# Twenty-two placements and orders for the two parts of a weight unit, in the half-steps of a macaron layer

## The chip, the cores and the metric

The kernel runs on one core of one Trainium2 chip (trn2). The metric is the device time of one execution in microseconds (us), the median of three runs. The engines of the core are named as in the profile: PE is the matrix engine and PEld its weight loads, DVE the vector engine, ACT the scalar engine, POOL the general engine, SP and ACT also issue the transfers.

## What is computed

One layer: a half-step SwiGLU feed-forward network (below: the first half-step), a token mixer of forgetting and stick-breaking attention with gated branches, and a second half-step of the same kind as the first. 16 meta tokens stand ahead of the 256 tokens and are dropped at the end. Everything is float32. Cut to the half-steps:

```
def _rmsnorm(x, gain):
    y = x32 * lax.rsqrt(jnp.mean(x32 * x32, axis=-1, keepdims=True) + RMS_EPS)
    return (y * gain).astype(x.dtype)
def _swiglu(x, w_gate, w_up, w_down):
    return (jax.nn.silu(x @ w_gate) * (x @ w_up)) @ w_down
...
h = h + 0.5 * _swiglu(_rmsnorm(h, ffn1_norm), ffn1_w_gate, ffn1_w_up, ffn1_w_down)
h = h + _hybrid_mixer(_rmsnorm(h, mix_norm), ...)
h = h + 0.5 * _swiglu(_rmsnorm(h, ffn2_norm), ffn2_w_gate, ffn2_w_up, ffn2_w_down)
```

The model width is 2048, the inner width 5632, so gate, up and down of one half-step hold 3 x 2048 x 5632 weights.

## The kernel before

**Parts.** A float32 product is made of three products of a faster type (float32r). Each operand is split into a high part (rounded) and a low part (the rest); high by high, high by low and low by high are added up in one accumulator, and low by low is left out. For weights the parts are the tiles `wh` and `wl`: ACT rounds (`act.activation(hi, src, AF.Copy)`, L164), DVE subtracts (L165).

**Units.** All weights are cut into units of 1024 columns by 128 partitions, 512 KB each: two blocks of 128 rows (`n` = 2) by 512 output features where a block is 512 wide. There are 264 units in the first half-step, then those of the mixer, then 264 in the second half-step. SP loads a unit up to six units ahead (`raw`, five buffers), `split_unit` makes its parts up to two units ahead (three buffers each of `wh` and `wl`, 4096 bytes a partition), and `products` (L917) issues its matmuls at L944. The order of the program is this loop; the lanes of generators that `tick()` moves on put the other work (norms, attention, transposes) between the matmuls. A scheduler of the language sets the final order from the program's order and its own estimate of when inputs are there.

**First half-step: by feature.** A matmul has 128 weights columns as stationary operand and 272 tokens (256 and 16 meta) of the activations as moving one. A unit has four outputs (`j`), two blocks of rows (`i`) and three terms, 24 matmuls. The four outputs have one of the eight accumulator banks each. The three terms of one `i` follow each other: `wh` with the activations' high part, `wh` with their low part, `wl` with their high part. The activations' parts lie in tiles of 2 x 2 x 272 (`tile_of`, L204): block, part, token. One row of 272 elements is 1088 bytes, 64 more than a multiple of 256, so the four rows of such a tile begin 0, 64, 128 and 192 bytes past a multiple of 256, counted from the tile's begin.

**Second half-step: by token.** Here the activations are stationary (128 tokens of a high or low part) and 512 weight columns are moving: two outputs, two blocks, three terms, 12 matmuls a unit, in the order (activations high, `wh`), (high, `wl`), (low, `wh`). The activations' tiles are 2 x 2 x 256 here, rows of 1024 bytes: all four begin at a multiple of 256 from the tile's begin.

**The mixer** has both kinds: by-feature blocks for queries, keys and values, and by-token blocks for the gates and the branches. The gates read the normalized activations in the tile of 272-token rows; the branches read the attention's outputs in tiles of 256-token rows. So the gates and the branches are the same matmuls (128 stationary columns, 512 moving ones) with other distances between the operands' begins.

**Where the tiles lie.** The built program has the activations' tiles (4352 bytes a buffer, 17 x 256), the `wh` and `wl` buffers and each of their halves all at one and the same rest from a multiple of 256 (192 bytes past it). In what follows the **distance** of a matmul is the rest by 256 of the moving operand's begin less the stationary one's. It is 0, 64, 0, 128, 192, 128 for the six matmuls of one output in the first half-step, and 0 for all of the second half-step and of the branches.

**The start.** `first_start` and `first_products` (L906) run ahead of the loop; the transposes there need the unit matrix `ident`, which POOL makes; `identr` and `onesr` are copies of `ident` and `ones` in float32r, made later (L136, L137).

**The end.** `down2` (L832) adds each finished output to the residual (DVE, L838) and sends it out (L841). In the last block each output is worked off in two halves.

Of the kernel before, what the change touches and what calls it, by code (L numbers as in the profile page):

```python
# [32 lines left out]
SPLIT_BUFS = 3  # L33
LOAD_AHEAD = 6
SPLIT_AHEAD = 2


class Block:
# [9 lines left out]
def hybrid_layer(ctx: ExitStack, tc: tile.TileContext, x, meta_tokens, ffn1_norm, ffn1_w_gate, ffn1_w_up,  # L48
# [47 lines left out]
            tick()  # L96


    ident = const([P, P], F32, "ident")
    make_identity(nc, ident)  # L100
    ones = const([P, P], F32, "ones")
    nc.gpsimd.memset(ones[:], 1.0)
    eps_c = const([P, 1], F32, "eps")
    nc.gpsimd.memset(eps_c[:], EPS)
    grow = const([64, P], F32, "grow")
    grow1 = const([16, P], F32, "grow1")
    nc.scalar.dma_start(grow1[:], ffn1_norm.rearrange("o (k p) -> (o k) p", p=P))
    for i, g in enumerate((ffn1_norm, mix_norm, ffn2_norm)):
# [7 lines left out]
    def tables():  # L116
        return tc.keep_in_program_order(act.preload_act_table_set(LN_EXP)).ins

    gcol1 = const([P, 16], F32, "gcol1")
    gcol = const([P, 64], F32, "gcol")  # L120
    gq = const([P, 8], F32, "gq")

    identr = const([P, P], F32R, "identr")
    onesr = const([P, P], F32R, "onesr")
# [5 lines left out]
    def other_constants():  # L130
        yield 8
        g_ps = aux()
        pe.transpose(g_ps[:, :64], grow[:], ident[:64, :64])
        dve.tensor_copy(gcol[:], g_ps[:, :64])
        dve.tensor_scalar(gq[:], gcol[:, 48:56], SCALE, None, op0=ALU.mult)
        tc.keep_in_program_order(dve.tensor_copy(identr[:], ident[:]))  # L136
        tc.keep_in_program_order(dve.tensor_copy(onesr[:], ones[:]))  # L137
        tc.keep_in_program_order(dve.tensor_scalar(negone[:], ones[:], -1.0, None, op0=ALU.mult))
# [54 lines left out]
    class Norm:  # L193
# [53 lines left out]
        def by_feature(self):  # L247

            n, ps = self.n, aux()
            pe.matmul(ps[:, :n], ones[:], self.acc[:, :n], start=True, stop=True)  # L250
# [43 lines left out]

    def first_gains():
        g_ps = aux()
        pe.transpose(g_ps[:, :16], grow1[:], ident[:16, :16])
        dve.tensor_copy(gcol1[:], g_ps[:, :16])

    def first_meta():  # L300
        p = aux()
        for h in range(2):
            pe.transpose(p[:, h * P:(h + 1) * P], ms[:, h, :], ident[:])
        t = p[:, :2 * P].rearrange("p (k t) -> p k t", t=NM)
        dve.tensor_tensor(mgain, t, gcol1[:].unsqueeze(2).to_broadcast([P, KT, NM]), op=ALU.mult)
        return t

    def first_transposes(c):
        ps = [aux(), aux()]
        for i in range(2):  # L310
            for j in range(2):
                pe.transpose(ps[i][:, j * P:(j + 1) * P], xs[c][:, j, i * P:(i + 1) * P], ident[:])  # L312
        return ps

    def first_parts(kt, p):
# [51 lines left out]
            act.activation(s[:], xs[c][:, j, :], AF.Square, accum_out=sums[:, j, c:c + 1])  # L367

    def meta_squares():
        dve.tensor_reduce(msel, ident[:].rearrange("p (k t) -> p t k", t=NM), axis=AX.X, op=ALU.add)  # L370
# [4 lines left out]
    def first_factors():  # L375
# [12 lines left out]
        rsqrt_newton(a[:], y[:], half[:])  # L388
        diag = temp([P, NT], F32, "half")
        for j in range(2):  # L390
            dve.tensor_scalar(diag[:, j * P:(j + 1) * P], ident[:], a[:, j:j + 1], None, op0=ALU.mult)
# [3 lines left out]
        pe.matmul(p[:, :NR], ones[:], diag[:, :NR], start=True, stop=True)  # L395
# [8 lines left out]
    def turn(u, dest, t0):  # L404

        yield 6
        for j0 in range(0, 4, 2):
            p = aux()
            for j in range(2):
                for i in range(2):  # L410
                    c = (j0 + j) * P
                    pe.transpose(p[:, (2 * j + i) * P:(2 * j + i + 1) * P], u[:, i, c:c + P], ident[:])  # L412
# [144 lines left out]
    def values(v):  # L557
        pv = aux()
        for i in range(3):
            pe.transpose(pv[:, i * P:(i + 1) * P], v[:, i * P:(i + 1) * P], ident[:])  # L560
# [83 lines left out]
    def fox_attend(h, t, parts):  # L644
# [23 lines left out]
        for kt in range(3):  # L668
            d = pb if kt == 2 else pa
            for i in range(2):  # L670
                c = (kt % 2) * NR + i * P
                pe.transpose(d[:, c:c + P], pw[:, i, kt * P:(kt + 1) * P], ident[:])  # L672
# [149 lines left out]
    def residual_by_token():  # L822
        for c in range(4):
            acc[c] = slot([P, 2, 512], F32)
            for i in range(2):
                ps = aux()
                for j in range(4):
                    pe.transpose(ps[:, j * P:(j + 1) * P], resid(4 * c + j)[:, i * P:(i + 1) * P], ident[:])  # L828
                dve.tensor_copy(acc[c][:, i, :], ps[:])
                yield 4  # L830

# [47 lines left out]
    def load(u):  # L879
# [3 lines left out]
        nc.sync.dma_start(t[:], b.w[rows, b.col0:b.col0 + b.cols].rearrange("(k p) c -> p k c", p=P))  # L883
        raws[u] = t

    def split_unit(u):
        b, k0, n = units[u]
        wh = wp.tile([P, n, b.cols], F32R, tag="wh", name=name("wh"))
        if b.stacked:
            raw, s = raws.pop(u), b.stacked  # L890
            act.activation(wh[:], raw[:], AF.Copy)
# [3 lines left out]
        wl = wp.tile([P, n, b.cols], F32R, tag="wl", name=name("wl"))  # L895
        split(wh[:], wl[:], raws.pop(u)[:])
        halves[u] = (wh, wl)

    def split_half(u, i):
        b, k0, n = units[u]  # L900
        if i == 0:
            halves[u] = tuple(wp.tile([P, n, b.cols], F32R, tag=t, name=name(t)) for t in ("wh", "wl"))
        wh, wl = halves[u]
        split(wh[:, i, :], wl[:, i, :], raws[u][:, i, :])

# [11 lines left out]
    def products(u):  # L917
# [8 lines left out]
        for j in range(outs):  # L926
            ps = banks[b][j]
            cs = slice(j * P, (j + 1) * P)
            for i in range(n):
                x = b.rhs(k0 + i)  # L930
                first, last = k0 + i == 0, k0 + i == b.kts - 1
                if b.by_token:
                    xh, xl = x[:, 0, cs], x[:, 1, cs]
                    terms = ((ps[:], xh, wh[:, i, :]), (ps[:], xh, wl[:, i, :]), (ps[:], xl, wh[:, i, :]))
                elif wide:
                    terms = ((ps[:].rearrange("p (a t) -> p a t", a=2), wh[:, i, cs], x[:, :, :NR]),
                             (ps[:, :NR], wl[:, i, cs], x[:, 0, :NR]))
                elif b.stacked:
                    terms = tuple((ps[:, :b.n], wh[:, i, cs], x[:, m, :b.n]) for m in range(2))
                else:  # L940
                    o, xh, xl = ps[:, :b.n], x[:, 0, :b.n], x[:, 1, :b.n]
                    terms = ((o, wh[:, i, cs], xh), (o, wh[:, i, cs], xl), (o, wl[:, i, cs], xh))
                for m, (o, a, c) in enumerate(terms):
                    pe.matmul(o, a, c, start=first and m == 0, stop=last and m == len(terms) - 1,  # L944
                              skip_group_check=wide)
# [99 lines left out]
```

## Time and profile before

| | us |
|---|---|
| median of 3 runs | 2248.3 (2248.03 to 2249.41) |
| the profiled execution | 2249.19 |
| its span | 2247.5 |
| PE busy | 2240.8 |
| DVE busy | 1265.4 |
| ACT busy | 1024.6 |

The span is the time from the program's first to its last instruction; the profiled execution took 1.7 us more than its span and 0.9 us more than the median. PE's records overlap, because a matmul is recorded until its last result is out while the next has begun. So the pace of matmuls is not their mean duration but a stretch of time divided by the matmuls that began in it.

### The profile page before, as it was taken

To read this page: it belongs to the slowest core of one execution; us is meant where nothing else is said; L and a number is where in the kernel's file an instruction comes from. 1 tells how busy PE (TensorE), PEld (TensorE's weight loads), DVE (VectorE), ACT (ScalarE), POOL (GpSimd) and SP (SyncE) were. 2 spreads that over 40 slices of the span, in tenths; PEclk is the share of its full clock that TensorE was granted. 3 is DMA by queue.
4 is the path that set the end of the run, shared out by engine and by line. 5 is a ranking of instruction groups with operands and counts; after the bars stand their busy time and mean duration, and the time that the engine had idled before them with its cause. 6 is when DMAs were issued, how large, how long until landed. Compare 5 with 4: busy or idle time off the path is not lost.

```text
span 2247.5 us, 34143 instructions
## 1 busy us (share of the span) xinstructions
PE 2240.8 (100%) x13930; PEld 2039.6 (91%) x13930; DVE 1265.4 (56%) x1596; ACT 1024.6 (46%) x1280; POOL 42.1 (2%) x112
## 2 busy tenths in 40 slices
PE   9999999999999999999999999999999999999999
PEld 9999999999999999988899988888888888888887
DVE  6555544455555555987556666675445544544554
ACT  6444433334444454655446564454444433444433
POOL 1000000000000001110000000000000000000000
PEclk9999999999999999999999999999999999999999
DMA  7666655566665566555655556566666666666664
GB/s 228 171 177 178 172 177 177 171 178 176 172 177 175 173 184 180 158 167 167 194 180 151 150 150 187 181 185 178 188 190 193 187 191 194 191 190 190 188 199 156
DMA packets 211325, 403.03 MB, mean 179 GB/s; under 512 B 12680, under 2 KB 17632, under 8 KB 211168
## 3 DMA queue, kind: packets, MB, share of 16 engines
q1 hardware_dynamic: 209088, 397.33, 59.1%
q8 instruction: 109, 1.79, 0.3%
q10 hardware_dynamic: 1472, 2.37, 0.3%
q0 software_dynamic: 608, 1.16, 0.2%
q14 instruction: 48, 0.39, 0.1%
HBM read 398.70 MB, written 2.11 MB: 178 GB/s over the span
## 4 chain that ended last, share of the span: by engine, by line
PE 99%; DMA 0%; SPq 0%; DVE 0%; issue 0%; DVEq 0%; ACT 0%
PE acc L944 96%; PE aux L701 1%; PE aux L572 1%; PE aux L412 1%; PE aux L672 0%; PE aux L560 0%; PE acc L914 0%; DMA v<-in_meta_tokens_dram 0%; PE aux L828 0%; PE aux L312 0%; PE aux L651 0%; PE aux L652 0%; PE aux L653 0%; PE aux L615 0%; PE aux L616 0%; PE aux L238 0%
## 5 line engine op out<-in xcount | busy, mean ns | idle before, releaser
L165 DVE TENSOR_TENSOR wl<-raw,wh 128x1024 fp32r<-128x1024 f32 (+1 forms) x753 | 921.4, 1224 | 857.3 <-ACT wh L164 855.8
L164 ACT ACTIVATE wh<-raw 128x1024 fp32r<-128x1024 f32 (+1 forms) x753 | 797.2, 1059 | 1096.2 <-PE acc L944 1029.7
L944 PE MATMUL acc<-v,wh 128*128 128x272 f32 (+1 forms) x5776 | 1172.9, 298 | 0.0
L944 PEld LDWEIGHTS acc<-v,wh 128*128 128x128 f32 x5776 | 923.6, 189 | 22.7
L944 PE MATMUL acc<-wh,v 128*128 128x512 f32 x2880 | 905.9, 391 | 0.0
L944 PE MATMUL acc<-v,wl 128*128 128x272 f32 (+1 forms) x3128 | 897.0, 287 | 0.0
L944 PEld LDWEIGHTS acc<-wh,v 128*128 128x128 f32 x2880 | 540.6, 188 | 111.7
L944 PEld LDWEIGHTS acc<-v,wl 128*128 128x128 f32 x3128 | 587.4, 188 | 0.4 <-DVE wl L165 0.2
L944 PE MATMUL acc<-wl,v 128*128 128x512 f32 x1440 | 561.3, 390 | 0.0
L944 PEld LDWEIGHTS acc<-wl,v 128*128 128x128 f32 x1440 | 270.5, 188 | 54.6
L164 ACT ACTIVATE v<-aux 128x512 fp32r<-128x512 f32 (+1 forms) x46 | 23.7, 516 | 19.2 <-PE aux L412 11.9
L165 DVE TENSOR_TENSOR v<-aux,v 128x512 fp32r<-128x512 f32 (+1 forms) x46 | 27.4, 595 | 4.3 <-ACT v L164 2.6
L440 DVE TENSOR_TENSOR sq<-acc,rbc 128x272 f32<-128x272 f32 x44 | 19.3, 438 | 18.5 <-PE acc L944 17.3
L431 DVE TENSOR_TENSOR v<-acc,rbc 128x272 f32<-128x272 f32 x44 | 18.0, 436 | 15.7 <-PE acc L944 15.7
L164 ACT ACTIVATE v<-sq 128x272 fp32r<-128x272 f32 x44 | 17.4, 419 | 19.5 <-DVE sq L441 19.5
L432 ACT ACTIVATE v<-v 128x272 f32<-128x272 f32 x44 | 17.5, 424 | 13.8 <-DVE v L431 13.8
L473 DVE SCALAR_TENSOR_TENSOR v<-acc,v 128x272 f32<-128x272 f32 x32 | 12.9, 435 | 12.6 <-PE acc L944 12.6
L441 DVE TENSOR_TENSOR sq<-sq,v 128x272 f32<-128x272 f32 x44 | 19.3, 438 | 0.8
L852 ACT ACTIVATE v<-acc,rtok 128x512 f32<-128x512 f32 x22 | 15.2, 690 | 9.9 <-PE acc L944 9.7
L412 PEld LDWEIGHTS aux<-ident,v 128*128 128x128 f32 x120 | 14.8, 140 | 3.7
L165 DVE TENSOR_TENSOR v<-sq,v 128x272 fp32r<-128x272 f32 x44 | 18.2, 434 | 0.0
L412 PE MATMUL aux<-ident,v 128*128 128x128 f32 x120 | 17.9, 272 | 0.0
(219 smaller groups left out, 725.7 us busy)
## 6 DMA issues: line engine op xcount, KB each, us to landing
raw<-in_ffn_w_up_dram SPq DMA_DIRECT2D x176, 512.0 KB, 3.7
raw<-in_ffn_w_down_dram SPq DMA_DIRECT2D x176, 512.0 KB, 3.9
raw<-in_ffn_w_gate_dram SPq DMA_DIRECT2D x175, 512.0 KB, 3.7
raw<-in_w_in_dram SPq DMA_DIRECT2D x162, 512.0 KB, 3.7
raw<-in_w_out_dram SPq DMA_DIRECT2D x32, 512.0 KB, 3.9
raw<-in_w_branch_fox_dram SPq DMA_DIRECT2D x16, 512.0 KB, 3.9
raw<-in_w_branch_sb_dram SPq DMA_DIRECT2D x16, 512.0 KB, 3.9
v<-in_x_dram SPq DMA_DIRECT2D x8, 256.0 KB, 7.8
```

The costliest lines, as they stand in the source:

```text
L164: act.activation(hi, src, AF.Copy)
L165: dve.tensor_tensor(lo, src, hi.bitcast(F32), op=ALU.subtract)
L412: pe.transpose(p[:, (2 * j + i) * P:(2 * j + i + 1) * P], u[:, i, c:c + P], ident[:])
L431: dve.tensor_tensor(s, ps[:, :n], norm_of().r[:, :n], op=ALU.mult)
L432: act.activation(s, s, AF.Silu)
L440: dve.tensor_tensor(u, ps[:, :n], norm_of().r[:, :n], op=ALU.mult)
L441: dve.tensor_tensor(u, u, s, op=ALU.mult)
L473: dve.scalar_tensor_tensor(r, ps[:, :NT], 0.5, r, op0=ALU.mult, op1=ALU.add)
L572: pe.matmul(po[:, :NR], a[:, ks], b[:, i * NR:(i + 1) * NR], start=n == 0, stop=n == 6)
L701: pe.matmul(o, a, b, start=start, stop=stop, skip_group_check=True)
L852: act.activation(u["t"][:, i, :], ps[:], AF.Silu, scale=norms["ffn2"].rtok[:, i:i + 1])
L944: pe.matmul(o, a, c, start=first and m == 0, stop=last and m == len(terms) - 1, skip_group_check=wide)
```

## The change

`WAYS` holds 22 ways for each half-step. A way has an order of the three terms, an offset in elements for `wh` and one for `wl` in their buffers, and whether a unit's outputs take turns. In an order, the first number of a pair is the weights' part and the second the activations' (0 high, 1 low); so `HHL` is high-high, high-low, low-high. `way(u)` gives every twelve units of a half-step the next way. The buffers grow from 1024 to 1088 elements (4352 bytes), and `part_tile` puts the part at the way's offset: 16 elements are 64 bytes. Where outputs take turns, `products` does the first matmul of every output, then the second of each, and so on, and finishes all outputs together at the end of the unit.

In the second half-step `HHL` means (`wh`, high), (`wh`, low), (`wl`, high), so the order of a by-token unit differs from the one before in all ways, and in the mixer's by-token blocks too, which take the first way of the list. Of the second half-step's ways 6 have both offsets zero, 10 have both offsets equal and not zero (64, 128 or 192 bytes), and 6 have two different offsets. Of the first half-step's ways 3 have offsets that are no multiples of 64 bytes. All tiles now begin 128 bytes past a multiple of 256, so the distances at offset zero are those of before.

Besides, the unit matrix and the ones are made by POOL in a temporary tile, and DVE copies them into `identr` and `onesr` at the start; `ident` and `ones` are these tiles read as float32. `grow1` and `gcol1` become slices of `grow` and `gcol`, with one small transfer less on POOL's queue.

```diff
+HHL = ((0, 0), (0, 1), (1, 0))
+LHH = ((1, 0), (0, 0), (0, 1))
+HLH = ((0, 1), (0, 0), (1, 0))
+WAYS = {
+    False: [(HHL, 0, 0, 0), (HHL, 32, 40, 0), (HHL, 32, 32, 0), (HHL, 48, 16, 0), (HHL, 16, 0, 0), (HHL, 40, 48, 0),
...
+    True: [(HHL, 0, 0, 0), (HHL, 16, 16, 0), (HHL, 32, 32, 0), (HHL, 48, 48, 0), (HHL, 0, 32, 0), (HHL, 32, 0, 0),
...
+PART = 1024 + 64
...
+    plain = temp([P, 2, NT], F32, "F3")
+    make_identity(nc, plain[:, 0, :P])
+    nc.gpsimd.memset(plain[:, 1, :P], 1.0)
...
     dve.memset(warm, 1.0)
+    dve.tensor_copy(identr[:], plain[:, 0, :P])
+    dve.tensor_copy(onesr[:], plain[:, 1, :P])
...
+    second = len(units) - 6 * FT
+    def way(u):
+        if u >= second:
+            return WAYS[True][(u - second) // 12]
+        return WAYS[False][u // 12 if u < mixer else 0] if not units[u][0].by_token else WAYS[True][0]
+
+    def part_tile(u, low):
+        b, k0, n = units[u]
+        tag = ("wh", "wl")[low]
+        t = wp.tile([P, PART], F32R, tag=tag, name=name(tag))
+        o = way(u)[1 + low]
+        return t[:, o:o + n * b.cols].rearrange("p (k c) -> p k c", k=n)
...
+        if in_turn:
+            for m in range(len(todo[0])):
+                for j in range(outs):
+                    multiply(j, m)
+        for j in range(outs):
+            ps = banks[b][j]
+            if not in_turn:
+                for m in range(len(todo[j])):
+                    multiply(j, m)
```

On PE, a unit in the middle of the second half-step before (`acc` is the accumulator, `wh` or `wl` moving, `v` the activations):

```order
L944 MATMUL acc_16704<-wh_16738,v_15595 128x512
L944 MATMUL acc_16704<-wl_16739,v_15595 128x512
L944 MATMUL acc_16704<-wh_16738,v_15595 128x512 x2
L944 MATMUL acc_16704<-wl_16739,v_15595 128x512
L944 MATMUL acc_16704<-wh_16738,v_15595 128x512
```

and one that comes near that place after, under `HHL`:

```order
L981 MATMUL acc_17326<-wh_17414,v_15836 128x512 x2
L981 MATMUL acc_17326<-wl_17415,v_15836 128x512
L981 MATMUL acc_17326<-wh_17414,v_15836 128x512 x2
L981 MATMUL acc_17326<-wl_17415,v_15836 128x512
```

The same six matmuls of one output stand there; `wl` has moved from the second to the third place.

On PE, the last unit of the program before, at the end of the second half-step:

```order
L944 MATMUL acc_20810<-wh_20928,v_20281 128x512
L944 MATMUL acc_20811<-wh_20928,v_20281 128x512
L944 MATMUL acc_20811<-wl_20929,v_20281 128x512
L944 MATMUL acc_20811<-wh_20928,v_20281 128x512 x2
L944 MATMUL acc_20811<-wl_20929,v_20281 128x512
L944 MATMUL acc_20811<-wh_20928,v_20281 128x512
```

and after (`LHH`, outputs in turn):

```order
L981 MATMUL acc_20806<-wh_20924,v_20277 128x512
L981 MATMUL acc_20807<-wh_20924,v_20277 128x512
L981 MATMUL acc_20806<-wl_20925,v_20277 128x512
L981 MATMUL acc_20807<-wl_20925,v_20277 128x512
L981 MATMUL acc_20806<-wh_20924,v_20277 128x512
L981 MATMUL acc_20807<-wh_20924,v_20277 128x512
L981 MATMUL acc_20806<-wh_20924,v_20277 128x512
L981 MATMUL acc_20807<-wh_20924,v_20277 128x512
```

Before, the first output is done six matmuls ahead of the second; after, one matmul ahead.

On PE, the first products before (`aux` with `ident` is a transpose of the activations' second tile, `v_122`):

```order
L914 MATMUL acc_201<-v_178,wl_182 128x272
L312 MATMUL aux_214<-ident,v_122 128x128 x2
L312 MATMUL aux_215<-ident,v_122 128x128 x2
L914 MATMUL acc_198<-v_178,wh_181 128x272
```

and after, where that tile is `v_120`:

```order
L947 MATMUL acc_196<-v_176,wh_179 128x272
L947 MATMUL acc_197<-v_176,wh_179 128x272
L947 MATMUL acc_198<-v_176,wh_179 128x272
L947 MATMUL acc_199<-v_176,wh_179 128x272
L330 MATMUL aux_212<-identr,v_120 128x128 x2
L947 MATMUL acc_196<-v_176,wh_179 128x272
```

The first of these transposes has moved from behind twelve products to behind four.

## Rows read from the trace of the kernel before

**Rows 1.** The page: span, then busy us, share of span, instructions.

```profile
span 2247.5 us, 34143 instructions
...
PE 2240.8 (100%) x13930; PEld 2039.6 (91%) x13930; DVE 1265.4 (56%) x1596; ACT 1024.6 (46%) x1280; POOL 42.1 (2%) x112
```

**Rows 2.** The page's 40 slices: granted clock of PE, in tenths.

```profile
PEclk9999999999999999999999999999999999999999
```

**Rows 3.** The waits of PE: us in total, times, longest.

```profile
PE aux L303 <- DMA v<-in_meta_tokens_dram: 1.4, 2, 0.8
PE aux L293 <- DVE v L276: 1.1, 1, 1.1
PE acc L914 <- ACT v L326: 0.3, 1, 0.3
```

**Rows 4.** First half-step, L944 alone: stretch, PE (matmuls), PEld (loads), clock, DMA.

```profile
60.00:800.00 740.00, 740.00 (x5896) 740.00 (x5895) 1.00 0.59 175
```

**Rows 5.** The chain in order of time (start, us): gates, branches, second half-step.

```profile
974.79 4.18 PE acc L944 x18
...
1325.19 8.29 PE acc L944 x36
...
1390.13 9.55 PE acc L944 x42
...
1787.33 172.78 PE acc L944 x762
```

**Rows 6.** The chain near the start: first products in turn, units in another order.

```profile
11.37 1.51 PE acc L914 x12
...
17.13 3.00 PE acc L944 x24
...
24.07 3.01 PE acc L944 x24
```

**Rows 7.** The page's groups: busy us, mean ns, idle before and its releaser.

```profile
L165 DVE TENSOR_TENSOR wl<-raw,wh 128x1024 fp32r<-128x1024 f32 (+1 forms) x753 | 921.4, 1224 | 857.3 <-ACT wh L164 855.8
L164 ACT ACTIVATE wh<-raw 128x1024 fp32r<-128x1024 f32 (+1 forms) x753 | 797.2, 1059 | 1096.2 <-PE acc L944 1029.7
...
L944 PEld LDWEIGHTS acc<-v,wl 128*128 128x128 f32 x3128 | 587.4, 188 | 0.4 <-DVE wl L165 0.2
```

**Rows 8.** The start in order of time: identity, warm-up, first transpose, first products.

```profile
1.19 0.29 POOL masks.py:199 TENSOR_SCALAR_AFFINE_SELECT ident<-ident 128x128 f32<-128x128 f32 x1
...
3.98 0.23 PE L297 MATMUL aux<-ident,grow 16*128 16x16 f32 x1
...
7.86 2.18 PE L914 MATMUL acc<-v,wh 128*128 128x272 f32 x8 [0.32 <-ACT v L326]
...
9.84 1.10 PE L914 MATMUL acc<-v,wl 128*128 128x272 f32 x4
```

**Rows 9.** One copy into a float32r constant: duration ns, first and last start us.

```profile
L136 DVE CAST identr<-ident x1: 223/223/223, 49.9 to 49.9; 128x128 fp32r<-128x128 f32 x1
```

**Rows 10.** The load of the second activation tile: duration ns, start, landing.

```profile
L280 SPq DMA_DIRECT2D v<-in_x_dram x1: 455/455/455, 2.8 to 2.8; - x1
...
DMA to landing us min/median/max: 5.7/5.7/5.7
```

**Rows 11.** The end in order of time: last matmul, its evacuation, the output's transfers.

```profile
2243.28 0.39 PE L944 MATMUL acc<-wh,v 128*128 128x512 f32 x1
2243.70 0.76 DVE L838 SCALAR_TENSOR_TENSOR v<-acc,v 128x256 f32<-128x256 f32 x2 [0.60 <-PE acc L944]
```

More of the change, by code (lines that the diff above doesn't have):

```diff
@@ L35 @@
 SPLIT_AHEAD = 2
+HHL = ((0, 0), (0, 1), (1, 0))
[3 more added lines that the diff above has]
+    False: [(HHL, 0, 0, 0), (HHL, 32, 40, 0), (HHL, 32, 32, 0), (HHL, 48, 16, 0), (HHL, 16, 0, 0), (HHL, 40, 48, 0),
+            (HHL, 0, 16, 0), (HHL, 8, 48, 0), (HHL, 48, 32, 0), (HHL, 16, 16, 0), (HHL, 48, 48, 0), (LHH, 0, 0, 0),
+            (LHH, 16, 16, 0), (LHH, 32, 32, 0), (LHH, 48, 48, 0), (HLH, 0, 0, 0), (HLH, 16, 16, 0), (HLH, 32, 32, 0),
+            (HLH, 48, 48, 0), (HHL, 0, 0, 1), (HHL, 32, 32, 1), (LHH, 16, 16, 1)],
+    True: [(HHL, 0, 0, 0), (HHL, 16, 16, 0), (HHL, 32, 32, 0), (HHL, 48, 48, 0), (HHL, 0, 32, 0), (HHL, 32, 0, 0),
+           (HHL, 0, 16, 0), (HHL, 16, 0, 0), (HHL, 0, 48, 0), (HHL, 48, 0, 0), (LHH, 0, 0, 0), (LHH, 32, 32, 0),
+           (LHH, 16, 16, 0), (HLH, 0, 0, 0), (HLH, 32, 32, 0), (HLH, 16, 16, 0), (HHL, 0, 0, 1), (HHL, 32, 32, 1),
+           (HHL, 16, 16, 1), (HLH, 0, 0, 1), (HLH, 32, 32, 1), (LHH, 0, 0, 1)]}
+PART = 1024 + 64
 class Block:
@@ L96, in drain @@
             tick()
[L99 to L102, printed above, removed]
+    identr = const([P, P], F32R, "identr")
+    ident = identr[:].bitcast(F32)
+    onesr = const([P, P], F32R, "onesr")
+    ones = onesr[:].bitcast(F32)
+    plain = temp([P, 2, NT], F32, "F3")
+    make_identity(nc, plain[:, 0, :P])
+    nc.gpsimd.memset(plain[:, 1, :P], 1.0)
     eps_c = const([P, 1], F32, "eps")
@@ L105, in hybrid_layer @@
     grow = const([64, P], F32, "grow")
-    grow1 = const([16, P], F32, "grow1")
-    nc.scalar.dma_start(grow1[:], ffn1_norm.rearrange("o (k p) -> (o k) p", p=P))
-    for i, g in enumerate((ffn1_norm, mix_norm, ffn2_norm)):
+    grow1 = grow[:16]
+    nc.scalar.dma_start(grow1, ffn1_norm.rearrange("o (k p) -> (o k) p", p=P))
+    for i, g in enumerate((mix_norm, ffn2_norm), 1):
         nc.gpsimd.dma_start(grow[16 * i:16 * i + 16, :], g.rearrange("o (k p) -> (o k) p", p=P))
@@ L133, in other_constants @@
         pe.transpose(g_ps[:, :64], grow[:], ident[:64, :64])
-        dve.tensor_copy(gcol[:], g_ps[:, :64])
+        dve.tensor_copy(gcol[:, 16:], g_ps[:, 16:64])
         dve.tensor_scalar(gq[:], gcol[:, 48:56], SCALE, None, op0=ALU.mult)
-        tc.keep_in_program_order(dve.tensor_copy(identr[:], ident[:]))
-        tc.keep_in_program_order(dve.tensor_copy(onesr[:], ones[:]))
-        tc.keep_in_program_order(dve.tensor_scalar(negone[:], ones[:], -1.0, None, op0=ALU.mult))
+        tc.keep_in_program_order(dve.tensor_scalar(negone[:], ones, -1.0, None, op0=ALU.mult))
         yield 4
@@ L249, in by_feature @@
             n, ps = self.n, aux()
-            pe.matmul(ps[:, :n], ones[:], self.acc[:, :n], start=True, stop=True)
+            pe.matmul(ps[:, :n], ones, self.acc[:, :n], start=True, stop=True)
             y = temp([P, NT], F32, "sq", bufs=2)[:, :n]
@@ L296, in first_gains @@
         g_ps = aux()
-        pe.transpose(g_ps[:, :16], grow1[:], ident[:16, :16])
-        dve.tensor_copy(gcol1[:], g_ps[:, :16])
+        pe.transpose(g_ps[:, :16], grow1, ident[:16, :16])
+        dve.tensor_copy(gcol1, g_ps[:, :16])
     def first_meta():
@@ L302, in first_meta @@
         for h in range(2):
-            pe.transpose(p[:, h * P:(h + 1) * P], ms[:, h, :], ident[:])
+            pe.transpose(p[:, h * P:(h + 1) * P], ms[:, h, :], ident)
         t = p[:, :2 * P].rearrange("p (k t) -> p k t", t=NM)
-        dve.tensor_tensor(mgain, t, gcol1[:].unsqueeze(2).to_broadcast([P, KT, NM]), op=ALU.mult)
+        dve.tensor_tensor(mgain, t, gcol1.unsqueeze(2).to_broadcast([P, KT, NM]), op=ALU.mult)
         return t
@@ L394, in first_factors @@
         p = aux()
-        pe.matmul(p[:, :NR], ones[:], diag[:, :NR], start=True, stop=True)
+        pe.matmul(p[:, :NR], ones, diag[:, :NR], start=True, stop=True)
         pe.matmul(p[:, NR:NT], ones[:NM, :], diag[:NM, NR:NT], start=True, stop=True)
@@ L884, in load @@
         raws[u] = t
+    second = len(units) - 6 * FT
+    mixer = next(u for u, (b, _, _) in enumerate(units) if b.w is wi)
+    def way(u):
[8 more added lines that the diff above has]
+        return t[:, o:o + n * b.cols].rearrange("p (k c) -> p k c", k=n)
     def split_unit(u):
         b, k0, n = units[u]
-        wh = wp.tile([P, n, b.cols], F32R, tag="wh", name=name("wh"))
+        wh = part_tile(u, 0)
         if b.stacked:
             raw, s = raws.pop(u), b.stacked
-            act.activation(wh[:], raw[:], AF.Copy)
+            act.activation(wh, raw[:], AF.Copy)
             dve.tensor_tensor(wh[:, :, 32:32 + s], raw[:, :, :s], wh[:, :, :s].bitcast(F32), op=ALU.subtract)
@@ L894, in split_unit @@
             return
-        wl = wp.tile([P, n, b.cols], F32R, tag="wl", name=name("wl"))
-        split(wh[:], wl[:], raws.pop(u)[:])
+        wl = part_tile(u, 1)
+        split(wh, wl, raws.pop(u)[:])
         halves[u] = (wh, wl)
@@ L901, in split_half @@
         if i == 0:
-            halves[u] = tuple(wp.tile([P, n, b.cols], F32R, tag=t, name=name(t)) for t in ("wh", "wl"))
+            halves[u] = tuple(part_tile(u, low) for low in range(2))
         wh, wl = halves[u]
@@ L925, in products, with terms @@
         wide = not b.by_token and b.n == NR
-        for j in range(outs):
+        order, _, _, in_turn = way(u)
+        w = wh, wl
+        def terms(j):
             ps = banks[b][j]
@@ L930, in products, with multiply @@
                 x = b.rhs(k0 + i)
-                first, last = k0 + i == 0, k0 + i == b.kts - 1
                 if b.by_token:
-                    xh, xl = x[:, 0, cs], x[:, 1, cs]
-                    terms = ((ps[:], xh, wh[:, i, :]), (ps[:], xh, wl[:, i, :]), (ps[:], xl, wh[:, i, :]))
+                    yield from ((ps[:], x[:, m, cs], w[l][:, i, :]) for l, m in order)
                 elif wide:
-                    terms = ((ps[:].rearrange("p (a t) -> p a t", a=2), wh[:, i, cs], x[:, :, :NR]),
-                             (ps[:, :NR], wl[:, i, cs], x[:, 0, :NR]))
+                    yield ps[:].rearrange("p (a t) -> p a t", a=2), wh[:, i, cs], x[:, :, :NR]
+                    yield ps[:, :NR], wl[:, i, cs], x[:, 0, :NR]
                 elif b.stacked:
-                    terms = tuple((ps[:, :b.n], wh[:, i, cs], x[:, m, :b.n]) for m in range(2))
+                    yield from ((ps[:, :b.n], wh[:, i, cs], x[:, m, :b.n]) for m in range(2))
                 else:
[L941 to L945, printed above, removed]
+                    yield from ((ps[:, :b.n], w[l][:, i, cs], x[:, m, :b.n]) for l, m in order)
+        todo = [list(terms(j)) for j in range(outs)]
+        def multiply(j, m):
+            o, a, c = todo[j][m]
+            pe.matmul(o, a, c, start=k0 == 0 and m == 0, stop=k0 + n == b.kts and m == len(todo[j]) - 1,
+                      skip_group_check=wide)
+        if in_turn:
[7 more added lines that the diff above has]
+                    multiply(j, m)
             if wide and k0 + n == b.kts:
```

18 lines of the change are left out of this document (8 added, 10 removed).

## Prediction

> **What bounds the kernel now.** I read the page's first part, its slices, the waits, and then the pace of the matmuls. PE is busy for 2240.8 of 2247.5 us, with 13930 matmuls and as many weight loads, while DVE and ACT are at about half [rows 1]. Its clock is at the full level, 2.4 GHz, in every slice [rows 2]. Its waits are a few us in all, and the longest rows lie in the start [rows 3]. So the span is a sum of matmuls, and a change does something only if it changes the time from one matmul's begin to the next one's. I call that the pace.
>
> The pace is longer than the columns need. In the first half-step 5896 matmuls begin in 740 us: 125.5 ns each [rows 4]. A matmul has 272 columns, which at 2.4 GHz are 113.3 ns, so 12.2 ns come on top. In the second half-step a stretch of 762 takes 172.78 us, 226.7 ns each [rows 5], against 213.3 ns for 512 columns: 13.4 ns on top. The on-top part is what this change can move. It is about 6336 x 12.2 = 77 us in the first half-step (264 units of 24) and 3168 x 13.4 = 42 us in the second (264 units of 12).
>
> Does it hang on where operands lie? The mixer has a comparison that nobody planned. Gates and branches are the same matmuls, by 128 stationary columns and 512 moving ones. In the gates the distances of the operands change, in the branches they are zero. An unbroken stretch of 36 gate matmuls takes 8.29 us, 230.3 ns each; 42 of the branches take 9.55 us, 227.4 ns each, near the 226.7 ns of the second half-step, whose distances are zero too [rows 5]. So 512 columns at mixed distances cost about 3.5 ns more than at distance zero. The costliest gate stretch, 18 in 4.18 us, is at 232.2 ns [rows 5]; it follows attention products and shows the upper end.
>
> **The change part by part.**
>
> *Second half-step, placement.* Six of 22 ways keep distance zero: 6 x 144 = 864 matmuls that should stay at 226.7 ns. Their new order of terms changes the stationary part at each step and not the distance, so I count it at nothing. The other 16 ways, 2304 matmuls, leave distance zero. The nearest row is the gates' 230.3 ns: 2304 x 3.5 ns = +8.1 us. In ten of these ways the distance is constant, which no row shows for 512 columns, so the bounds are wide. The upper bound is the gates' worst, 232.2 - 226.7 = 5.5 ns, +12.7 us. The lower one is below nothing: the on-top part was 11.7 ns in one stretch of 24 matmuls (3.00 us, 125.0 ns each, less 113.3) [rows 6], and with that 512 columns would take 225.0 ns, 2304 x -1.7 = -3.9 us. I take the gates', because they are the same instruction at other distances.
>
> *First half-step, placement and order.* Here the distances are mixed already: all four occur in every six matmuls. A displacement of both parts by 128 bytes (one way) only swaps the two blocks' rôles, and the first way is the old one. That leaves 20 ways, 5760 matmuls, in other mixtures. Three rows show the same instruction in another order: the first products, where four outputs take turns, 12 in 1.51 us, 125.8 ns; and two start-up units in which the high parts of all four outputs come first, 24 in 3.00 and in 3.01 us, 125.0 and 125.4 ns [rows 6]. All lie within half a ns of the 125.5 of rows 4. I take 0, with bounds of 5760 x -0.5 = -2.9 us and 5760 x +0.3 = +1.7 us. The offsets that are no multiple of 64 bytes (three ways) have no row; I put them inside these bounds.
>
> *Splits and buffers.* ACT and DVE write the same elements at another place: 1059 and 1224 ns a unit [rows 7], beside a unit's 24 x 125.5 = 3012 ns or 12 x 226.7 = 2720 ns on PE. With `LHH` PE wants `wl`, the last thing made, first. In the old order the loads of `wl` sat idle for 0.4 us in all 3128 [rows 7], and a unit is split up to two units ahead, so the cover is over 2.7 us and the cost nothing. Were it gone, 1.2 us would be lost in each unit of the nine `LHH` ways; nothing points there.
>
> *The start.* The two copies cost 223 ns each on DVE [rows 9]. POOL's identity is done at 1.48 us and PE first reads it at 3.98 [rows 8], so the 0.45 us lie in a gap of 2.5 us: nothing, and 0.45 us without that cover. The transposes of the second activation tile now stand behind four products instead of twelve. Eight products take 9.84 - 7.86 = 1.98 us there, so four end about 7.86 + 0.99 = 8.85 us [rows 8]; the tile is issued at 2.8 and lands 5.7 us later, at 8.5 [rows 10]. PE need not wait, by a margin of 0.35 us; if the load is late by more, PE and the products behind it wait for it. I count 0, between -0.4 and +0.4 us. The small transfer that POOL's queue loses is read by nobody early.
>
> *The end.* The last way lets both outputs take turns. Before, the first output was worked off beside the six matmuls of the second. Now it is ready one matmul (0.23 us) ahead of it, and DVE needs 0.76 us for an output's two halves [rows 11], so the second output's begin slips by 0.76 - 0.23 = 0.53 us: +0.5 us, with no cover, since nothing follows. Block ends inside the half-steps finish their outputs together too, but the next block has other accumulator banks: nothing.
>
> *The mixer.* Its 768 gate matmuls get another order at the same distances. Between 230.3 and 232.2 ns [rows 5] that is at most 1.5 us either way; I take 0.
>
> The sum against the profiled execution: 2249.2 + 8.1 + 0.5 = 2257.8 us. The median of before is 0.9 us lower than that execution, so the forecast for the median is 2256.9, told as 2257.
>
> **A rule that speaks against it.** The rows above show a pace that differs with distance, 227.4 against 230.3 ns [rows 5]. The Trainium skill, "TensorE: Matmul & The Clock Gate", Part 2, says that loading the next weights does not steal read bandwidth from the running matmul, because PE has two independent read ports; by that rule placement is free, and this trace does not agree as far as gates and branches go. The same page, "Back-to-back issue gap", gives N/2.4 + 2.5 ns for full clock, an estimate of 215.8 ns for 512 columns; the row has 226.7.
>
> **The rivals.**
>
> *A constant distance is as good as none.* The gates change distance from matmul to matmul; ten ways do not. If only the change costs, six ways pay: 6 x 144 x 3.5 = 3.0 us, and the median is 2248.3 + 3.0 + 0.5 = 2251.8. For it: the steadiest pace of the trace is where nothing changes. Against it: no row has a constant distance other than zero.
>
> *Placement does nothing*, and the gates are slow for the attention products between them: 2248.3 + 0.5 = 2248.8 us. This is what the rule above would give. Against it: the 36 gate matmuls of 8.29 us have nothing between them.
>
> *Other distances are faster on the whole.* This is the other side of zero. Mixed distances of the first half-step have less on top of the columns (12.2 ns) than distance zero has in the second (13.4 ns). If leaving zero brings the 11.7 ns of the best stretch to both half-steps, the sum is -3.9 - 2.9 + 0.5 = -6.3, and the median is 2242.0. It decides from the point where 16 ways of the second half-step fall below 226.7 ns. Against it stand the gates again.
>
> *All is as dear as the worst gates*: +12.7 + 1.7 + 0.5 gives 2263.2 us.
>
> **How the numbers follow.** The forecast has 0.50, the constant distance 0.17, no effect 0.10, faster 0.13, the worst gates 0.10. About 0.2%, 4.5 us, can be told from no change here. The forecast and the worst gates are slower by more than that, save for some 0.02 at the forecast's lower edge: 0.58. The constant distance, no effect and that edge are within: 0.29. Faster is 0.13. The range leaves out most of the faster case and whatever lies beyond the worst gates: 2245 to 2264.
>
> **What would show it.** In the profile after, the second half-step should have twelve-unit stretches (about 33 us each) at 226.7 ns where offsets are zero and near 230 ns elsewhere, and the first half-step should stay within half a ns of 125.5 at every way. A stretch at constant non-zero distance that runs at 226.7 would refute the main term, one below 226 would make the third rival right. First half-step stretches at 122 or 129 ns would show that mixtures differ more than the three rows say, with 0.7 us for each way and 2.5 ns. PE waits for `wl` in the `LHH` ways would show the split's cover gone.

## The result and the profile after

| | before | after |
|---|---|---|
| median, us (4 runs each) | 2248.24 (2248.03 to 2249.41) | 2259.69 (2259.47 to 2259.90) |
| ratio | | 1.005, 95% interval 1.0032 to 1.0067 |
| span of the profiled execution, us | 2247.5 | 2258.2 |

The kernel became slower by 11.45 us, 0.5%. The forecast was 2257, a loss of 8.6 us by the sum of its steps.

The page of the kernel after, its first rows and its granted clock (they answer to [rows 1] and [rows 2]):

```profile
span 2258.2 us, 34152 instructions
...
PE 2250.7 (100%) x13930; PEld 2036.9 (90%) x13930; DVE 1267.4 (56%) x1596; ACT 1023.4 (45%) x1280; POOL 41.1 (2%) x111
...
PEclk9999999999999999999999999999999999999999
```

The same 13930 matmuls, the same full clock in every slice: what changed is again only the pace. The waits of PE after (total, times, longest; they answer to [rows 3]), and the split's two groups from the page ([rows 7]):

```profile
PE aux L321 <- DMA v<-in_meta_tokens_dram: 1.2, 2, 0.6
PE aux L311 <- DVE v L292: 1.1, 1, 1.1
PE acc L947 <- ACT v L344: 0.3, 1, 0.3
PE aux L330 <- DMA v<-in_x_dram: 0.3, 1, 0.3
```

```profile
L181 DVE TENSOR_TENSOR wl<-raw,wh 128x1024 fp32r<-128x1024 f32 (+1 forms) x753 | 921.4, 1224 | 862.1 <-ACT wh L180 857.7
...
L981 PEld LDWEIGHTS acc<-v,wl 128*128 128x128 f32 x3128 | 574.8, 188 | 0.4 <-DVE wl L181 0.2
```

No wait for `wl` appeared under `LHH`: the same 0.4 us of idle time as before. The splits take what they took, 1224 ns. One wait is new, 0.3 us for the second activation tile.

The chain of waits after (start, us, what; it answers to [rows 5]). In order: the long stretch of the first half-step, 36 gate matmuls, 42 branch matmuls, and the long stretch of the second half-step:

```profile
48.69 765.45 PE acc L981 x6100
...
1323.72 8.37 PE acc L981 x36
...
1389.39 9.55 PE acc L981 x42
...
1791.54 175.47 PE acc L981 x762
```

The long stretch of the second half-step rose from 172.78 to 175.47 us for the same 762 matmuls, 226.7 to 230.3 ns each. The 36 gate matmuls rose from 8.29 to 8.37 us, and the branches, still at distance zero, kept their 9.55. The first half-step became shorter; before, the same stretch was

```profile
49.05 768.05 PE acc L944 x6100
```

Cut by stage, from the chain's starts, the first matmul of the second half-step (begun at 1510.41 us before, 1509.66 after) and the last one (2243.28 before, 2253.43 after):

| stage | us after less before |
|---|---|
| to the begin of the 6100 | 48.69 - 49.05 = -0.4 |
| the 6100 of the first half-step | 765.45 - 768.05 = -2.6 |
| mixer | (1509.66 - 814.14) - (1510.41 - 817.10) = +2.2 |
| second half-step, from its begin to the last matmul's begin | (2253.43 - 1509.66) - (2243.28 - 1510.41) = +10.9 |
| the end | (2258.20 - 2253.43) - (2247.49 - 2243.28) = +0.6 |
| sum, the span's difference | +10.7 |

**Way by way.** Inside one way the chain, asked for a short window, gives pure stretches. The second half-step after, eight ways in order of time; the offsets and orders are, from the top, `HHL` (16, 16), `HHL` (32, 32), `HHL` (32, 0), `HHL` (16, 0), `LHH` (0, 0), `LHH` (32, 32), `HLH` (16, 16), and `HLH` (0, 0) with outputs in turn:

```profile
1548.96 13.28 PE acc L981 x58
...
1582.87 24.64 PE acc L981 x106
...
1700.79 13.28 PE acc L981 x58
...
1753.88 29.17 PE acc L981 x125
...
1854.83 30.37 PE acc L981 x134
...
1887.99 30.10 PE acc L981 x129
...
2021.90 28.15 PE acc L981 x123
...
2156.96 28.11 PE acc L981 x124
```

Divided, these are 229.0, 232.5, 229.0, 233.4, 226.6, 233.3, 228.9 and 226.7 ns. The distance sets the pace here, whatever the order and whether outputs take turns: zero is at 226.7 in the fifth and eighth row, (16, 16) at 229 in the first and seventh, (32, 32) at 232.5 to 233.3 in the second and sixth. Summed by way from the begins of the matmuls, the 10.9 us are 4.3 in the five ways of (32, 32), 0.96 in the one of (48, 48), 1.2 in the four of (16, 16), 4.2 in the six with two different offsets, and 0.2 in the six at zero.

The first half-step after, four ways in order of time: `HHL` (32, 32), `HHL` (8, 48), `HLH` (0, 0), and the last way, `LHH` (16, 16) in turn:

```profile
89.92 30.13 PE acc L981 x240
...
267.95 30.12 PE acc L981 x242
...
557.95 30.15 PE acc L981 x238
...
774.90 30.11 PE acc L981 x242
```

That is 125.5, 124.5, 126.7 and 124.4 ns: where before every way had 125.5, there are five steady paces now by the begins of the matmuls, 124.45, 124.8, 125.0 (at (48, 16)), 125.55 and 126.7, in sum a gain.

The end, in order of time (start, us, engine; it answers to [rows 11]):

```profile
2252.75 1.07 PE L981 MATMUL acc<-wh,v 128*128 128x512 f32 x4
...
2253.63 1.42 DVE L856 SCALAR_TENSOR_TENSOR v<-acc,v 128x256 f32<-128x256 f32 x4 [5.62 <-PE acc L981]
```

Four half-outputs now stand behind the last matmuls, 1.42 us of DVE; before, two stood there with 0.76 us.

### The profile page after: what moved, and what is told of

It reads as the page before. It is cut to its first block, busy times and chain, and to the rows that moved or that the text cites. A ratio compares the mean times of both kernels' runs of the same rounds, so it can differ in the third digit from the quotient of the medians.

```text
span 2258.2 us, 34152 instructions
## 1 busy us (share of the span) xinstructions
PE 2250.7 (100%) x13930; PEld 2036.9 (90%) x13930; DVE 1267.4 (56%) x1596; ACT 1023.4 (45%) x1280; POOL 41.1 (2%) x111
## 4 chain that ended last, share of the span: by engine, by line
PE 99%; DMA 0%; ACT 0%; DVE 0%; SPq 0%; issue 0%; DVEq 0%; ACTq 0%
PE acc L981 96%; PE aux L719 1%; PE aux L590 1%; PE aux L430 1%; DMA v<-in_x_dram 0%; PE aux L690 0%; PE aux L578 0%; PE aux L846 0%; ACT wh L180 0%; PE aux L330 0%; PE aux L633 0%; PE aux L669 0%; PE aux L670 0%; PE aux L671 0%; PE aux L634 0%
## 5 line engine op out<-in xcount | busy, mean ns | idle before, releaser
L181 DVE TENSOR_TENSOR wl<-raw,wh 128x1024 fp32r<-128x1024 f32 (+1 forms) x753 | 921.4, 1224 | 862.1 <-ACT wh L180 857.7
L981 PE MATMUL acc<-v,wh 128*128 128x272 f32 (+1 forms) x5776 | 1145.6, 298 | 0.1
L981 PEld LDWEIGHTS acc<-v,wh 128*128 128x128 f32 x5776 | 905.5, 188 | 23.3 <-ACT wh L180 0.6
L981 PE MATMUL acc<-wh,v 128*128 128x512 f32 x2880 | 877.9, 394 | 0.0
L981 PE MATMUL acc<-v,wl 128*128 128x272 f32 (+1 forms) x3128 | 859.4, 287 | 0.0
L981 PEld LDWEIGHTS acc<-v,wl 128*128 128x128 f32 x3128 | 574.8, 188 | 0.4 <-DVE wl L181 0.2
L981 PE MATMUL acc<-wl,v 128*128 128x512 f32 x1440 | 542.4, 393 | 0.0
L192 DVE TENSOR_TENSOR R<-F,R 128x512 fp32r<-128x512 f32 x16 | 11.0, 690 | 12.8 <-ACT R L191 12.7
L430 PEld LDWEIGHTS aux<-identr,v 128*128 128x128 f32 x120 | 14.7, 140 | 3.4
L430 PE MATMUL aux<-identr,v 128*128 128x128 f32 x120 | 17.5, 272 | 0.0
```

The lines of the kernel that those rows point to most:

```text
L181: dve.tensor_tensor(lo, src, hi.bitcast(F32), op=ALU.subtract)
L192: dve.tensor_tensor(lo[:, :n], src[:, :n], hi[:, :n].bitcast(F32), op=ALU.subtract)
L981: pe.matmul(o, a, c, start=k0 == 0 and m == 0, stop=k0 + n == b.kts and m == len(todo[j]) - 1, skip_group_check=wide)
```

## The experiments

All start from the kernel after, and each is compared with the kernel before on the same chip. `OLD` is the by-token order before, ((0, 0), (1, 0), (0, 1)). The theory was that the distance sets the pace of the second half-step; the rivals were that the new orders of the terms do it, that the layout of buffers and the start do it, and that the place of the weights in memory does it, whatever the activations' place.

**Orders alone.** All offsets zero, the 22 orders and turns kept.

```diff
...
-    True: [(HHL, 0, 0, 0), (HHL, 16, 16, 0), ...
+    True: [(HHL, 0, 0, 0)] * 10 + [(LHH, 0, 0, 0)] * 3 + [(HLH, 0, 0, 0)] * 3 + [(HHL, 0, 0, 1)] * 3
+          + [(HLH, 0, 0, 1)] * 2 + [(LHH, 0, 0, 1)]}
```

> All offsets zero; the orders of the terms and the turns stay as in the change (ways of one order stand together). Theory (the pace hangs on the distance, the order alone costs nothing in the second half-step): second half-step 226.7 ns in all ways, its 3168 matmuls about 719 us as before; the gates, whose order is changed, keep their +2.0 us; the first half-step loses 4 x 288 x 1.1 ns = 1.3 us in the HLH ways (126.7 ns there) and stays at 125.5 ns elsewhere; with +0.5 us at the end the median is 2251 to 2252 us. Rival (order or turns make a good part of the loss): second half-step 3 us or more longer than before, median above 2255.

Measured: 2251.06 us (2250.86 to 2252.3) against 2249.28, ratio 1.0009 (0.9999 to 1.0018), not to be told from no change by the medians alone. The chain: first half-step, 36 gate matmuls, second half-step, and, from a window inside the `HLH` ways, a stretch of the first half-step (the second line in time):

```profile
49.49 768.07 PE acc L977 x6100
...
559.93 30.13 PE acc L977 x240
...
1327.13 8.37 PE acc L977 x36
...
1790.03 172.75 PE acc L977 x762
```

The second half-step is back at 172.75 us, so orders and turns cost nothing there. The gates keep their 8.37 us, so their loss is the order's: from each of the 768 begins to PE's next one, 180.2 us in all against 178.2 before, +2.0 us (0.3 of it stands in the control below too). A miss: `HLH` in the first half-step has 125.5 ns here, not the 126.7 it had in the kernel after at the same offsets of zero. Way and offsets were the same; what stood before it was not.

**Offsets alone.** The offsets of the change, with the old orders and no turns.

```diff
+OLD = ((0, 0), (1, 0), (0, 1))
...
-    True: [(HHL, 0, 0, 0), (HHL, 16, 16, 0), ... (LHH, 32, 32, 0), ... (LHH, 0, 0, 1)]}
+    True: [(OLD, 0, 0, 0), (OLD, 16, 16, 0), ... (OLD, 32, 32, 0), ... (OLD, 0, 0, 0)]}
```

> All offsets as in the change, but the orders of before everywhere, no turns. Theory: second half-step +9 to +11 us (ways at zero 226.7 ns, at 64 bytes 229, at 128 and 192 bytes 232 to 234), gates as before (177.2 us, not 179.2), first half-step about 3 to 4 us shorter; median 2254 to 2256. Rival (order makes a good part): second half-step less than +6 us, median below 2252.

Measured: 2257.19 us (2257.03 to 2257.39), ratio 1.0035 (1.0022 to 1.0047). The expected 2254 to 2256 is missed by 1.2 us: the second half-step lost 10.9, at the upper end, and the first gained 2.6 instead of 3 to 4. The same places of its chain:

```profile
48.42 765.46 PE acc L977 x6100
...
1322.26 8.29 PE acc L977 x36
...
1789.28 175.48 PE acc L977 x762
```

The stretch of the second half-step is that of the kernel after to 0.01 us, and the first half-step's gain is here too. The gates are back at 8.29 us. So offsets make the loss of the second half-step and the gain of the first, orders make the loss in the gates. That the totals of the first half-step agree to 0.01 us is chance, though: by the begins, (16, 16) ran at 124.8 ns in two of its later ways here, and in the kernel after at 125.55 as the `LHH` and 124.45 as the `HLH` in their places. The ways ahead of those had the same offsets but other orders too, so a way's own order and what stood before it are not told apart there.

**The control.** Zero offsets, old orders, no turns: what is left are the larger buffers, the constants and the start.

```diff
...
+OLD = ((0, 0), (1, 0), (0, 1))
+WAYS = {False: [(HHL, 0, 0, 0)] * 22, True: [(OLD, 0, 0, 0)] * 22}
```

> The control: all offsets zero, orders of before, no turns; what is left of the change is the longer buffers, the constants made in another way and the other base of the tiles. Theory: same as before within 0.1%, 2247.5 to 2249.5 us, every stage at its old pace. Rival (the longer buffers or the start cost or gain something): over 2 us either way.

Measured: 2248.91 us against 2249.44, ratio 1.0001 (0.9991 to 1.0010). Its chain:

```profile
48.29 768.05 PE acc L975 x6100
...
1786.90 172.75 PE acc L975 x762
```

Both half-steps have the old pace, and the gates take 0.3 us more than before (178.5 us by their begins). So larger buffers, the copies of the constants and the earlier transposes cost nothing that can be measured.

**Move the activations after the weights.** All weights of the second half-step at (32, 32). The normalized activations, which gate and up read, are moved by the same 32 elements; the products, which down reads, are not. The mixer stays at zero.

```diff
...
+WAYS = {False: [(HHL, 0, 0, 0)] * 22, True: [(OLD, 32, 32, 0)] * 22}
...
-                self.parts.append(slot([P, 2, 2, self.n], F32R))
+                if self.wide:
+                    self.parts.append(slot([P, 2, 2, self.n], F32R))
+                else:
+                    t = slot([P, PART], F32R)
+                    self.parts.append(t[:, 32:32 + 1024].rearrange("p (k m t) -> p k m t", k=2, m=2))
```

> Orders of before everywhere. In the second half-step every weight part is displaced by 128 bytes; the normalized activations that gate and up read (2112 matmuls) are displaced by 128 bytes too, the inner activations that down reads (1056) are not. Theory (only the distance of the two operands counts): gate and up at 226.7 ns as before, down at 232 to 233.5 ns, second half-step +6 to +7 us, median 2253.5 to 2255.5. Rival (the place of the weights itself counts, by whatever writes or reads them): all at 232 to 233.5 ns, +18 to +21 us, median above 2265. Rival (only changes of distance cost, not a constant one): no more than +1 us.

Measured: 2255.71 us (2254.64 to 2256.6), ratio 1.0029 (1.0018 to 1.0040). Two stretches of its chain, the first in a down block, the second in gate and up:

```profile
1849.80 30.43 PE acc L979 x131
...
1915.79 30.37 PE acc L979 x134
```

The same weights at the same offset run at 232.3 ns where the activations stay, and at 226.6 where they have moved along. So neither the place of the weights by itself nor the splits that write there cost anything: it is the distance of the two operands. The Trainium skill, "TensorE: Matmul & The Clock Gate", Part 2, says that loading the next stationary operand takes no read bandwidth from the running matmul. Read as a rule on time, it would make the two rows alike; they are 5.7 ns apart, and so far this trace does not agree.

**Twenty-two distances.** Second half-step, both offsets equal, in steps of 4 elements (16 bytes) from 0 to 60, then 62, 2 and 1, and three pairs; the first half-step with other pairs, the mixer's by-feature blocks at (48, 32).

```diff
...
+    True: [(OLD, 0, 0, 0), (OLD, 4, 4, 0), (OLD, 8, 8, 0), (OLD, 12, 12, 0), ... (OLD, 60, 60, 0), ... (OLD, 0, 8, 0)]}
```

> A measuring kernel: orders of before, no turns; every twelve units of each half-step another pair of offsets, in steps down to 4 bytes. In the second half-step both parts are displaced alike in 19 ways (0, 4, 8 to 60, 62, 2, 1 elements). Theory: the pace is a function of the distance with 226.7 ns at 0, 229 at 16, 232 to 233 at 32 and 233 at 48 elements, and steps between them no finer than 4 elements; nothing below 226. Rival: some distance other than zero is faster than 226. In the first half-step 124.4 to 126.7 ns for all pairs; the mixer's by-feature blocks all take (48, 32) here, and their 272-column blocks should run at 124.5 instead of 125.56 ns (-1.7 us).

One execution, 2260.74 us. Stretches of its chain at 12, 44, 60 and 1 elements:

```profile
1614.86 28.29 PE acc L977 x123
...
1884.80 29.40 PE acc L977 x126
...
2020.82 29.24 PE acc L977 x129
...
2122.96 24.20 PE acc L977 x102
```

These are 230.0, 233.3, 226.7 and 237.3 ns. By the begins of their matmuls all others but zero itself lie between 229.0 and 234.6 ns, 4 elements at 231.7 and 2 at 232.2 among them. Nothing is below zero's 226.7, and the price does not grow with the distance. That steps would be no finer than 4 elements is refuted: one element is the dearest distance of this run. 60 elements, as good as zero here, is taken up again below. In the first half-step the best pace was 124.45 ns again, at (8, 48), (0, 8), (8, 0) and (12, 44); (48, 32), which had it in the kernel after, stood at the start here and shows none of its own.

**The best of each.** First half-step and the mixer's by-feature blocks at (48, 32), all else at zero and in the old order.

```diff
...
+OLD = ((0, 0), (1, 0), (0, 1))
+WAYS = {False: [(HHL, 48, 32, 0)] * 22, True: [(OLD, 0, 0, 0)] * 22}
```

> Orders of before, no turns; second half-step, gates and branches at offset zero; first half-step and the mixer's by-feature blocks all at (48, 32). Theory (distance sets the pace in each stage by itself): first half-step 6336 x (125.56 - 124.45) = -7.0 us, the mixer's 272-column blocks -1.5 us, its 512/256 pairs -1.7 us, the rest as before; median about 2238 us, ratio 0.9955. Rival (the 124.45 ns hold only for twelve units after some other way, since one placement was seen at two paces): first half-step at 125 ns or above in most of its ways, median above 2243.

Measured: 2239.13 us (2238.9 to 2240.98) against 2249.44, ratio 0.9958 (0.9946 to 0.9971). Its chain:

```profile
48.36 761.33 PE acc L975 x6100
...
1777.18 172.75 PE acc L975 x762
```

The first half-step is 6.7 us shorter than in the kernel before over the same 6100 matmuls, 124.45 ns by the begins in every way behind the first (over the 740 us of [rows 4] it was 125.5), and the second has kept its pace. From the end of the 6100 to the begin of the 762 it is (1777.18 - 809.69) - (1787.33 - 817.10) = -2.7 us, and -3.1 against the control. That is left to the by-feature blocks of the mixer: nothing else in that stretch differs from the control. This version beats both kernels; its median is 0.4% below the one before and some 20 us below the kernel after.

**The gates.** Each of the eight gate blocks with an order or offset of its own, in the order of the program: `OLD`, `HHL`, `LHH`, `HLH` at zero, then `OLD` at 16, 32, 48 and 60 elements.

```diff
...
+GATES = [(OLD, 0, 0, 0), (HHL, 0, 0, 0), (LHH, 0, 0, 0), (HLH, 0, 0, 0),
+         (OLD, 16, 16, 0), (OLD, 32, 32, 0), (OLD, 48, 48, 0), (OLD, 60, 60, 0)]
...
+        if b.by_token and b.kts == KT:
+            return GATES[gate_blocks.index(b)]
```

> First half-step all at (8, 48); the eight gate blocks of the mixer each another way: four orders at offset zero (that of before, HHL, LHH, HLH), then the order of before at 16, 32, 48 and 60 elements. Theory (what costs in the gates is the change of the distance between matmuls that follow each other, four changes in six under the order of before, six under HHL): LHH, with four changes, as before at 230 to 231 ns; HLH too; HHL 233.3 ns. Offsets in the gates: no better than zero, 230 to 234 ns, since they have all four rows of the activations in them. Rival (the order of before is a lucky one): LHH and HLH at 232 ns or more. First half-step at 124.45 ns.

One execution, 2240.41 us. One stretch of the chain from each of the first four blocks:

```profile
970.86 4.15 PE acc L982 x18
...
1002.26 4.17 PE acc L982 x18
...
1020.65 4.15 PE acc L982 x18
...
1038.47 5.58 PE acc L982 x24
```

By these, 230.6, 231.7, 230.6 and 232.5 ns. The stretches are short and begin behind attention products; from matmul begins that have at least ten gate matmuls ahead of them the means are 230.9, 233.1, 230.3 and 232.3, and 231.5 to 232.1 for `OLD` at the four offsets. The control, with `OLD` at zero in all, has 231.0, 231.6, 231.2 and 230.6 in the same first four blocks, so `HHL` and `HLH` cost 1.5 and 1.7 ns in their places and `LHH` nothing. So order matters where distances are mixed. That it is the number of changes of distance falls: `OLD`, `LHH` and `HLH` change it four times in six matmuls, `HHL` each time, and `HLH` is dear too. What in the order costs stays open.

**What stood before.** First half-step: (16, 16) by turns with (32, 32), later with (0, 0). Second: 60 elements behind several others, distance zero behind several others, and 58, 59, 61 and 63 elements.

```diff
...
+    False: [(HHL, 32, 32, 0), (HHL, 16, 16, 0)] * 6 + [(HHL, 0, 0, 0), (HHL, 16, 16, 0)] * 5,
+    True: [(OLD, 32, 32, 0), (OLD, 60, 60, 0), (OLD, 63, 63, 0), (OLD, 60, 60, 0), ... (OLD, 0, 0, 0), (OLD, 60, 60, 0), ...
```

> A measuring kernel, orders of before, no turns. First half-step: (16, 16) six times behind (32, 32), then five times behind (0, 0). It was seen at 124.8 ns four times behind (0, 0) and once behind (48, 32), and at 126.7 ns once behind (32, 32). Theory (the way before decides which of two steady paces a placement falls into): 126.7 ns in all six stretches behind (32, 32), 124.8 ns in all five behind (0, 0). Rival (chance, or the place in the program): both paces in both groups. Second half-step: distance zero comes five times behind other distances and should be at 226.7 ns each time once settled; the distance 240 bytes (60 elements), seen once at 226.8 ns, comes five times: at 226.8 ns always if the pace hangs on the distance alone, elsewhere too if on the way before.

One execution, 2267.03 us. Stretches of the chain, in order of time: first half-step, (16, 16) behind (32, 32); (16, 16) behind (0, 0); second half-step, 60 elements behind (32, 32); 60 behind (0, 0):

```profile
51.95 34.07 PE acc L977 x269
...
487.93 32.08 PE acc L977 x257
...
1554.96 12.54 PE acc L977 x53
...
1975.07 14.94 PE acc L977 x64
```

One and the same way of the first half-step runs at 126.7 or 124.8 ns, steady for its whole 36 us, by what ran before: six times of six behind (32, 32), five of five behind (0, 0). Here the six all stand ahead of the five, so the place in the program is a rival; the experiment with offsets alone answers it. It too has (16, 16) as its last way, but behind (32, 32), and there it runs at 126.6 ns, where the last way of this kernel has 124.8:

```profile
771.92 30.14 PE acc L977 x238
```

In the second half-step 60 elements runs at 236.6 and 233.4 here, and ran at 226.7 behind 56 elements in the sweep; that was another place in the program, which no run separates. Of the other distances 61 elements was the dearest of all, 239 ns by its begins. Distance zero settled at 226.7 ns behind each of the five ways that stood ahead of it. This fits the miss of the first experiment, where `HLH` at zero stood behind a way at (0, 0) and in the kernel after behind one at (48, 48); that pair itself was not run apart.

## Why the prediction was right, and where it was off

**The main term: right mechanism, too small.** The forecast counted 2304 matmuls at 3.5 ns, +8.1 us; measured were +10.9. The step that was off is the price taken from the gates' row: the gates are a mixture of distances whose pace in the old order, 230.3 ns, is not that of a single one. Constant distances of 128 and 192 bytes cost 6.0 and 6.7 ns (4.3 us over 720 matmuls, 0.96 over 144), 64 bytes cost 2.1 (1.2 over 576), and the ways with two offsets 4.8 on the whole (4.2 over 864). The upper bound, 5.5 ns from the costliest gate stretch, is passed by the two dearest groups, but not by the sum: 10.9 lies between the forecast and that rival.

**Order at distance zero costs nothing: right.** The first experiment shows it in all orders, 172.75 us for 762.

**A constant distance as good as none: refuted.** (32, 32) and (48, 48) are the dearest constant ways. **Placement does nothing: refuted** by the second experiment, and by the fourth in one and the same kernel. **Other distances faster: refuted in the second half-step**, where nothing fell below 226.7 ns; half of its argument held, though, since the first half-step did gain.

**First half-step at 0, bounds -2.9 and +1.7 us: measured -2.6.** The bound held, the middle did not, and the sign to be expected stayed unseen. The step that failed took three short rows of the start as a sample of what other mixtures do. They gave 125.0 to 125.8 ns, while the steady paces are 124.45 to 126.7; at 124.45 all the way it is worth 6.7 us, as the best version shows, over twice the lower bound. The text had named the sign of this error (stretches away from 125.5).

**Gates at 0, at most 1.5 us: measured +2.0.** This step failed by more than its bound, because the bound was a spread of rows in one order. The new order's mean is 233.2 ns a matmul against 230.7 before, by the begins of all 768 with the 13 gaps of over 300 ns left out in each kernel.

**The end: right.** +0.5 us forecast, 0.6 measured, with the mechanism of the rows: DVE's 1.42 us in place of 0.76.

**The start: as bounded.** The margin of 0.35 us for the earlier transposes was not there: the four products ended at 8.50 us, not at 8.85, and PE waited 0.3 us for the tile. Yet the stretch of 6100 began 0.4 us earlier. That beginning lay between 48.15 and 49.87 us among the profiles of all these kernels, so the 0.4 can't be given to the change. Splits, buffers and constants were hidden, as counted; the control shows it.

The errors in part cancelled: +2.8 in the second half-step, -2.6 in the first, +2.2 in the mixer, -0.4 and +0.1 at the ends make the 2.1 us by which the span grew more than forecast. The total came closer than its terms did, and that part is luck.

## What to carry to other kernels

Where matmuls with a weight load each bound a kernel, compare the pace with the columns' time, and look at the begins of both operands by 256 bytes: equal rests were the floor for 512 moving columns here, a tile moved without its partner cost 1 to 6% at all but one of the distances run (240 bytes, which was free once). For an operand whose rows can't all be aligned, a few offsets tried over stretches of 30 us each in one run are a cheap search (here 6.7 us in one half-step), but try the winner alone afterwards, since a stretch can inherit its pace from the one before.

## What the runs showed that was not expected

- A pace that hangs on what ran before: the same instructions at the same distances hold 124.8 or 126.7 ns for 36 us, and 226.7, 233.4 or 236.6 ns at 60 elements. Each is steady; what makes PE fall into one or the other is open.
- The price of two distances is no sum. With (32, 0) two matmuls of three are 128 bytes off and the pace is 229.0 ns; with (0, 32) only one of three is, and it is 233.3. Each stood behind one other pair only, so a part of history in this is not excluded.
- Why a distance costs at all is not shown. The rows tell that it needs both operands (the experiment that moved the activations) and that neither the order of the terms nor the splits take part at distance zero; whether reads of the two operands meet somewhere was argued only.
